# VectorE takes all element-wise work of a two-block network kernel from GpSimd; rotary tables and feed-forward operands are made at other places

## The chip, the cores and the metric

The kernel runs on one core of one Trainium2 chip: TensorE (PE, matrix products into PSUM), VectorE (DVE), ScalarE (ACT), GpSimd (POOL), and SyncE (SP), which issues most DMAs. The metric is the device time of one execution in microseconds, the median of several.

## The reference

Everything is fp32, with 512 tokens of width 1024. Cut to what matters (`first_block` is two layers, then `second_block` once):

```python
for l in range(2):
    x = x + 0.5 * swiglu(rmsnorm(x, g_ffn1[l]), wg1[l], wu1[l], wd1[l])      # d_ff = 2816
    u = rmsnorm(x, g_mix[l]); p = u @ w_in[l]
    y_a, y_b, y_c = fourier(p), dilated_attention(p), diff_attention(p)
    x = x + (gates(u) * (y_a, y_b, y_c)).sum() @ w_out[l]
    x = x + 0.5 * swiglu(rmsnorm(x, g_ffn2[l]), wg2[l], wu2[l], wd2[l])
x = rmsnorm(x, g_final)
# second block
proj = rms_norm(x, g_mix_pre) @ w_in_2
attn = window_attention(rope(aq), rope(ak), av)          # 8 heads, 2 kv heads
q, k, v = silu(conv5(dqkv)); q, k = l2norm(q), l2norm(k)  # 4 heads of 128
dn = gated_delta(q, k, v, g, beta) + flip(gated_delta(flip(q, k, v, g, beta)))
x = x + rms_norm([attn, gated(dn)] @ w_out_2, g_mix_post)
x = x + rms_norm(cross_attention(rms_norm(x), rms_norm(mem)), g_cross_post)
x = x + rms_norm(swiglu2(rms_norm(x, g_ffn_pre)), g_ffn_post)
```

## The kernel before, in words

The activations lie transposed: `self.x[c]`, c = 0 to 7, holds 128 channels x 512 tokens. Each fp32 product is made of three matmuls: every operand is split into a rounded part `hi` and a rest `lo` (`split`: ScalarE copies `hi`, VectorE subtracts to get `lo`), and hi·hi, hi·lo and lo·hi are summed in PSUM. Weights come as slabs of 512 KB (`raw`), are split in the same way into `whi` and `wlo`, and TensorE takes them in order.

The kernel is written as tasks (Python generators). `drive` picks the next task by priority and due time; `note` keeps an estimated clock for each engine (per instruction 0.065 + 0.00105 n us on VectorE, 0.17 + 0.00075 n on ScalarE, 0.1 + 0.0027 n on GpSimd, n the elements of a partition) and `when` gives the estimated time at which a tile is done. So the order of each engine's instructions comes from these estimates, and an instruction that is given to another engine moves others too. Each engine then works through its own list in order. One helper records every operation, so that all rows of the profile have one line, L119; the names tell them apart: `g` is any general tile of 128x512, `sm` a small one, `ps` a PSUM bank.

Places that the change touches:

- `split_w` (line 310) splits weight slabs. While `pool_w` is on (second mixer and cross attention), every second `lo` is subtracted on GpSimd.
- `sq_pool` (464) sums squares for a norm: at each new chunk of x a square (ScalarE) and an addition (GpSimd).
- `ffn_task` (821): hidden tiles 0 to 5 are made the plain way, tiles 6 to 21 by a fast scheme that makes a 2x2 block product from seven smaller ones. Its x operands 1 to 7 come from `fast_ops` (722): eight subtractions `g<-b` or `g<-b,g`, each split, in one go between the hidden tiles 4 and 5.
- `setup_second` (1389) makes the rotary tables `sin` and `cos` from the positions after the fourth feed-forward's fast part (`rooms == 4`), beside the chunks of the norm after it (`pre_chunk` with `G_FINAL`).
- `final_norm` (1440): finishes that norm, then multiplies the 8 chunks of x by 1/rms on GpSimd and stores them.
- In `mixer2_task` (1646), `conv`: for q and v heads two of five taps go over ScalarE and GpSimd. `gs` is the decay strength of the gated delta rule, which TensorE needs for cumulative sums (`strengths`); `l2_heads` normalises the K heads (`g<-ps,sm`).
- `delta_k`, `delta` and `rope` have multiplications on GpSimd; so have `post_task`, `post_halves` (norms after the mixer and the cross attention) and `finish`.
- `memory_proj` (2312) loads the normed memory from `mem_d` over GpSimd's DMA queue and starts its product 5 us (planner's time) later.

Of the kernel before, what the change touches and what calls it, by code (L numbers as in the profile page):

```python
# [135 lines left out]
class Net:  # L136
    def __init__(self, ctx, tc, ins, dump=None):
# [21 lines left out]
        self.pool_w = self.turn = False  # L159
# [161 lines left out]
    def slab(self, src, kc, c, whole=False):  # L321
# [142 lines left out]
    def sq_pool(self, k, x):  # L464
# [7 lines left out]
        if k == len(self.acc):  # L472
            self.acc.append(q)
        else:
            nc.gpsimd.tensor_tensor(self.acc[k], self.acc[k], q, ALU.add)

    def wide(self, srcs, us, first=4):
# [4 lines left out]
        for k in range(KC):  # L482
            if k % 4 == 0:
                self.lock, self.ahead = self.cur, True
                n = first if k == 0 else 4
                for j, src in enumerate(srcs):
# [235 lines left out]
    def fast_ops(self, xn, xr):  # L722
# [3 lines left out]
        ops = [None] * 8  # L726
        for i, r, sl in ((1, 0, one), (2, 1, one), (3, 1, two)):
            ops[i] = [(xr[2 * k + r][0][:, sl], xr[2 * k + r][1][:, sl]) for k in range(KC // 2)]
        for i in (4, 5, 6, 7):
            ops[i] = []  # L730
        for q in range(2):
            b11, b12, b21, b22 = (xn[r][q][:, :, sl] for r in range(2) for sl in (one, two))
            t = []
            for i, a, b in ((5, b12, b11), (6, b22, None), (7, b22, b12), (4, b21, None)):
                b = t[(i == 4)] if b is None else b
                t.append(self.g(shape=[P, 2, 256]))
                sub(a, b)
                hi, lo = self.split(t[-1], self.g(F32R, [P, 2, 256]), self.g(F32R, [P, 2, 256]))
                ops[i] += [(hi[:, k], lo[:, k]) for k in range(2)]
        return ops  # L740
# [80 lines left out]
    def ffn_task(self, wg, wu, wd, pre, row, after):  # L821
# [31 lines left out]
        xs = self.fast_ops(xn, xr)  # L853
# [32 lines left out]
        down(0, 6, (0,))  # L886
        load(0)
# [501 lines left out]
    def setup_second(self):  # L1389
# [27 lines left out]
        k = self.g()
        big = 12582912.0
        nc.vector.tensor_scalar(k, ang, 1.0 / (2.0 * math.pi), big, ALU.mult, ALU.add)
        nc.vector.tensor_scalar_add(k, k, -big)  # L1420
        c1 = 6.28125
        c2 = math.floor((2.0 * math.pi - c1) * 2.0 ** 20) / 2.0 ** 20
        c3 = 2.0 * math.pi - c1 - c2
        for c in (c1, c2, c3):
            nc.vector.scalar_tensor_tensor(ang, k, -c, ang, ALU.mult, ALU.add)
        nc.vector.tensor_scalar(k, ang, 1.0 / (2.0 * math.pi), big, ALU.mult, ALU.add)
        nc.vector.tensor_scalar_add(k, k, -big)
        for c in (c1, c2 + c3):
            nc.vector.scalar_tensor_tensor(ang, k, -c, ang, ALU.mult, ALU.add)
        lim = 3.1415925  # L1430
        nc.vector.tensor_scalar(ang, ang, -lim, lim, ALU.max, ALU.min)
        self.sin = self.pcst([P, S], "sin")
        nc.scalar.activation(self.sin, ang, AF.Sin)
        nc.vector.tensor_scalar_mul(self.sin, self.sin, self.m_sgn)
        nc.scalar.activation(ang, ang, AF.Abs)
        nc.vector.tensor_scalar(ang, ang, -1.0, 0.5 * math.pi, ALU.mult, ALU.add)
        self.cos = self.pcst([P, S], "cos")
        nc.scalar.activation(self.cos, ang, AF.Sin)

    def final_norm(self, a1, a2):  # L1440
# [19 lines left out]
        for c in range(KC):  # L1460
            nc.gpsimd.tensor_tensor(self.x[c], self.x[c], r1b, ALU.mult)
# [5 lines left out]
    def post_task(self, row, res, nxt, done):  # L1467
# [13 lines left out]
        for c in range(1, KC, 2):  # L1481
            nc.gpsimd.tensor_tensor(ms[c], ms[c], rb, ALU.mult)
# [55 lines left out]
    def post_halves(self, row, res, nxt, half, done):  # L1538
# [22 lines left out]
        def chunks(n, cs, p=None):  # L1561
            sl = slice(256 * n, 256 * n + 256)
            for c in cs:
                if c % 2:
                    nc.gpsimd.tensor_tensor(ms[c][:, sl], ms[c][:, sl], rbs[n], ALU.mult)
            for c in cs:
# [32 lines left out]
    def wide_halves(self, srcs):  # L1599
# [5 lines left out]
        for k in range(0, KC, 4):  # L1605
            w.append([])
            for j, src in enumerate(srcs):
# [3 lines left out]
                for c in range(2):  # L1611
# [5 lines left out]
                    w[-1].append(self.split_w(raw[:, :, c * P:(c + 1) * P], hi, lo))  # L1617
# [28 lines left out]
    def mixer2_task(self, after):  # L1646
# [6 lines left out]
        self.pool_w = True  # L1653
# [15 lines left out]
        def conv(p, x, h):  # L1669
# [997 lines left out]
```

## Time and profile before

| | us |
|---|---|
| median of 3 runs | 3449.83 (3449.82 to 3457.95) |
| profiled execution | 3453.07 |
| its span | 3451.3 |
| TensorE busy | 3320.4 (96%), x19063 |
| VectorE busy | 2297.5 (67%), x4180 |
| ScalarE busy | 1572.5 (46%), x3064 |
| GpSimd busy | 360.2 (10%), x372, 241 of them two-operand arithmetic |

TensorE's matmuls are 83% of the chain that ended last. The stretches that the text speaks of: the first feed-forward up to 172 us; mixers and feed-forwards to 2408; the last down product of the fourth feed-forward, the norm after it and the first product of the second mixer to 2494; the second mixer to 2924; its norm and the cross attention to 3096; the last feed-forward to the end. In a timeline the arrow names what ended an engine's wait; "x4" at a row means four like instructions in a row, and the time is that of all four.

### The profile page before, as it was taken

To read this page: it belongs to the slowest core of one execution; us is meant where nothing else is said; L and a number is where in the kernel's file an instruction comes from. 1 tells how busy PE (TensorE), PEld (TensorE's weight loads), DVE (VectorE), ACT (ScalarE), POOL (GpSimd) and SP (SyncE) were. 2 spreads that over 40 slices of the span, in tenths; PEclk is the share of its full clock that TensorE was granted. 3 is DMA by queue.
4 is the path that set the end of the run, shared out by engine and by line. 5 is a ranking of instruction groups with operands and counts; after the bars stand their busy time and mean duration, and the time that the engine had idled before them with its cause. 6 is when DMAs were issued, how large, how long until landed. Compare 5 with 4: busy or idle time off the path is not lost.

```text
span 3451.3 us, 50657 instructions
## 1 busy us (share of the span) xinstructions
PE 3320.4 (96%) x19063; PEld 2910.4 (84%) x19063; DVE 2297.5 (67%) x4180; ACT 1572.5 (46%) x3064; POOL 360.2 (10%) x372
## 2 busy tenths in 40 slices
PE   8899999999999999999999999999879888999998
PEld 6799888898899988998888988999667877888887
DVE  5677677656577777776775566777778674754344
ACT  4354545443444554544454434445454254443232
POOL 2000100000100010001000000000454412220001
PEclk9999999999999999999999999999989999999999
DMA  4443332435333333333333357333255623223332
GB/s 131 129 128 92 117 96 92 133 106 181 95 104 108 110 113 107 111 92 117 94 97 119 115 182 141 116 97 97 73 185 171 204 62 104 68 74 99 96 98 73
DMA packets 370949, 391.03 MB, mean 113 GB/s; under 512 B 30801, under 2 KB 325309, under 8 KB 370704
## 3 DMA queue, kind: packets, MB, share of 16 engines
q1 hardware_dynamic: 329248, 332.45, 32.1%
q10 hardware_dynamic: 38464, 47.68, 4.9%
q0 software_dynamic: 2992, 7.67, 0.7%
q8 instruction: 149, 2.44, 0.3%
q14 instruction: 96, 0.79, 0.1%
HBM read 343.56 MB, written 39.98 MB: 111 GB/s over the span
## 4 chain that ended last, share of the span: by engine, by line
PE 83%; DVE 7%; issue 2%; DMA 2%; ACT 1%; POOL 1%; SPq 0%; ACTq 0%; DVEq 0%; POOLq 0%
PE ps L119 83%; DVE g L119 5%; ACT g L119 1%; DVE wlo L119 1%; DVE sm L119 1%; DMA g<-cs_d 0%; POOL g L119 0%; DMA g<-g 0%; DMA g<-xinv_d 0%; SPq L119 0%; DVE tmp L119 0%; DMA b<-in_w_ffn_up 0%; ACT whi L119 0%; DMA g<-mem_d 0%; DMA g<-bias_d 0%
## 5 line engine op out<-in xcount | busy, mean ns | idle before, releaser
L119 PE MATMUL ps<-g,whi 128*128 128x512 f32 (+1 forms) x9312 | 2418.1, 350 | 36.3 <-ACT g L119 20.4
L119 PEld LDWEIGHTS ps<-g,whi 128*128 128x128 f32 x9312 | 1626.7, 191 | 259.8 <-ACT g L119 26.5
L119 PE MATMUL ps<-g,wlo 128*128 128x512 f32 (+1 forms) x4656 | 1619.4, 348 | 14.3 <-DVE wlo L119 14.1
L119 ACT ACTIVATE whi<-raw 128x512 fp32r<-128x512 f32 (+1 forms) x1084 | 669.7, 622 | 881.0 <-PE ps L119 786.5
L119 PEld LDWEIGHTS ps<-g,wlo 128*128 128x128 f32 x4656 | 888.7, 191 | 126.8 <-DVE wlo L119 16.5
L119 DVE TENSOR_TENSOR wlo<-raw,whi 128x512 fp32r<-128x512 f32 (+1 forms) x1022 | 704.0, 696 | 391.9 <-ACT whi L119 376.2
L119 ACT ACTIVATE g<-g 128x256 fp32r<-128x256 f32 (+4 forms) x561 | 311.5, 571 | 217.2 <-DVE g L119 182.1
L119 DVE TENSOR_TENSOR g<-g,g 128x512 f32<-128x512 f32 (+4 forms) x550 | 349.3, 655 | 88.7 <-ACT g L119 78.2
L119 POOL TENSOR_TENSOR g<-g,g 128x512 f32<-128x512 f32 (+3 forms) x142 | 179.6, 1273 | 1571.0 <-ACT g L119 1467.2
L119 DVE TENSOR_TENSOR g<-ps,g 128x512 f32<-128x512 f32 (+3 forms) x350 | 204.3, 598 | 197.0 <-PE ps L119 99.6
L119 PE MATMUL ps<-g,g 128*128 128x128 f32 (+5 forms) x1638 | 268.2, 312 | 23.7 <-DVE g L119 11.4
L119 PEld LDWEIGHTS ps<-g,g 128*128 128x128 f32 (+3 forms) x1638 | 226.5, 195 | 46.1 <-DVE g L119 11.5
L119 PE MATMUL ps<-whi,g 128*128 128x256 f32 (+1 forms) x1184 | 256.9, 310 | 0.1
L119 ACT ACTIVATE whi<-b 128x512 fp32r<-128x512 f32 x192 | 121.2, 632 | 223.6 <-PE ps L119 212.5
L119 DVE SCALAR_TENSOR_TENSOR g<-ps,g 128x512 f32<-128x512 f32 x210 | 149.1, 711 | 105.5 <-PE ps L119 103.4
L119 PEld LDWEIGHTS ps<-whi,g 128*128 128x128 f32 x1184 | 196.8, 192 | 11.8 <-ACT whi L119 0.4
L119 PE MATMUL ps<-wlo,g 128*128 128x256 f32 (+1 forms) x592 | 183.8, 311 | 5.8 <-DVE wlo L119 4.8
L119 DVE TENSOR_TENSOR wlo<-b,whi 128x512 fp32r<-128x512 f32 x192 | 131.8, 688 | 55.1 <-ACT whi L119 54.5
L119 ACT COPY g<-ps 128x512 f32<-128x512 f32 (+5 forms) x250 | 114.0, 476 | 118.2 <-PE ps L119 105.8
L119 ACT ACTIVATE g<-ps 128x256 fp32r<-128x256 f32 (+6 forms) x239 | 100.5, 430 | 144.3 <-PE ps L119 126.2
L119 DVE TENSOR_TENSOR g<-g,ps 128x512 f32<-128x512 f32 (+1 forms) x171 | 111.4, 656 | 40.7 <-PE ps L119 34.8
L119 PEld LDWEIGHTS ps<-wlo,g 128*128 128x128 f32 x592 | 113.6, 192 | 12.5 <-DVE wlo L119 5.6
(201 smaller groups left out, 1849.7 us busy)
## 6 DMA issues: line engine op xcount, KB each, us to landing
raw<-in_w_ffn_down SPq DMA_DIRECT2D x80, 512.0 KB, 3.5
raw<-in_w_in SPq DMA_DIRECT2D x80, 512.0 KB, 3.9
raw<-in_w_ffn_gate SPq DMA_DIRECT2D x55, 512.0 KB, 3.9
raw<-in_w_ffn_up SPq DMA_DIRECT2D x55, 512.0 KB, 4.4
raw<-in_w_gate SPq DMA_DIRECT2D x48, 512.0 KB, 3.7
raw<-in_w_gate_up SPq DMA_DIRECT2D x44, 512.0 KB, 3.6
b<-in_w_ffn_gate SPq DMA_DIRECT2D x32, 512.0 KB, 3.8
b<-in_w_ffn_up SPq DMA_DIRECT2D x32, 512.0 KB, 3.9
```

What stands on the lines that cost most here:

```text
L119: r = f(*a, **k)
```

## The change

All element-wise work of GpSimd goes to VectorE: `split_w` is replaced by `split`, and the additions and multiplications of the functions above are written for `nc.vector`. GpSimd keeps memsets and DMA issues. The convolutions of q and v heads do all five taps as K heads did (one ScalarE scaling, four VectorE multiply-adds). `fast_ops` makes its operands in two calls, the first at the old place, the second as an item of the list of the fast scheme, behind the first down slab. The rotary tables are made during the fourth feed-forward, in the tiles `sin` and `cos` themselves, a few instructions every 8 us of the planner's time. `memory_proj` waits 20 us instead of 5 between its loads and its product. The core of the diff:

```diff
-    def split_w(self, src, hi, lo):
-        self.nc.scalar.activation(hi, src, AF.Copy)
-        self.turn = self.pool_w and not self.turn
-        (self.nc.gpsimd if self.turn else self.nc.vector).tensor_tensor(lo, src, hi.bitcast(F32), ALU.subtract)
-        return hi, lo
...
-            self.split_w(q[4], hi, lo)
+            self.split(q[4], hi, lo)
...
-            nc.gpsimd.tensor_tensor(self.acc[k], self.acc[k], q, ALU.add)
+            nc.vector.tensor_tensor(self.acc[k], self.acc[k], q, ALU.add)
...
-        xs = self.fast_ops(xn, xr)
+        xs = [[] for _ in range(8)]
+        self.fast_ops(xn, xr, xs, 0)
         evac(5, self.proj_t(sg, P, xr), self.proj_t(su, P, xr), False)
...
         down(0, 6, (0,))
+        items.append((lambda: self.fast_ops(xn, xr, xs, 1), None))
         load(0)
...
-        yield lambda: self.rooms == 4
-        pi = self.g(I32)
-        nc.gpsimd.dma_start(pi, i["positions_2"][0].partition_broadcast(P))
-        yield 16.0
+        ang, k = self.pcst([P, S], "sin"), self.pcst([P, S], "cos")
+        nc.gpsimd.dma_start(k.bitcast(I32), i["positions_2"][0].partition_broadcast(P))
+        yield 40.0
...
+            yield 8.0
+            nc.vector.tensor_scalar(k, ang, 1.0 / (2.0 * pi), big, ALU.mult, ALU.add)
...
         for c in range(KC):
-            nc.gpsimd.tensor_tensor(self.x[c], self.x[c], r1b, ALU.mult)
+            nc.vector.tensor_tensor(self.x[c], self.x[c], r1b, ALU.mult)
...
-            for j in (1, 3) if pool else (0, 1, 3, 4):
+            for j in (0, 1, 3, 4):
...
-        nc.gpsimd.tensor_tensor(v3(rv), v3(rv), be3, ALU.mult)
-        nc.gpsimd.tensor_tensor(v3(kg), v3(kg), self.b3(self.kgs[c]), ALU.mult)
+        nc.vector.tensor_tensor(v3(rv), v3(rv), be3, ALU.mult)
+        nc.vector.tensor_tensor(v3(kg), v3(kg), self.b3(self.kgs[c]), ALU.mult)
...
-        yield 5.0
+        yield 20.0
         w = i["w_ckv_2"][0]
```

VectorE's list in the first feed-forward, before: `g_845<-ps_820,g_845` is the product of the hidden tile f = 5, `b_490` and `b_492` are normed x, the `g<-b` rows with the rows `g<-g,g` after them are the subtractions and splits of `fast_ops`.

```order
L119 TENSOR_TENSOR g_780<-g_777,g_779 128x512
L119 TENSOR_TENSOR g_783<-b_492,b_490 128x512
L119 TENSOR_SCALAR bgh<-par 128x48
L119 TENSOR_SCALAR slg<-par 128x1 x2
L119 TENSOR_TENSOR g_786<-g_783,g_785 128x512
L119 TENSOR_TENSOR g_789<-b_492,g_777 128x512
L119 TENSOR_TENSOR wlo_911<-raw_900,whi_910 128x512
L119 TENSOR_TENSOR g_792<-g_789,g_791 128x512
L119 TENSOR_TENSOR wlo_915<-raw_890,whi_914 128x512
L119 TENSOR_TENSOR g_845<-ps_820,g_845 128x512
L119 TENSOR_TENSOR g_850<-g_845,g_849 128x512
```

The same place after; `g_821<-ps_796,g_821` is the product of f = 5 here, and `g_866<-b_490` the first row of the second step.

```order
L119 TENSOR_TENSOR g_768<-g_765,g_767 128x512
L119 TENSOR_TENSOR wlo_903<-raw_898,whi_902 128x512
L119 TENSOR_TENSOR raw_894<-raw_894,b_896 128x1024
L119 TENSOR_TENSOR g_821<-ps_796,g_821 128x512
L119 COPY par<-ps_829 128x128
L119 TENSOR_TENSOR wlo_907<-raw_898,whi_906 128x512
L119 TENSOR_TENSOR g_826<-g_821,g_825 128x512
L119 TENSOR_SCALAR bgh<-par 128x48
L119 TENSOR_TENSOR g_835<-g_740 128x256
L119 TENSOR_SCALAR slg<-par 128x1 x2
L119 TENSOR_REDUCE sm_837<-g_835 128x4
L119 TENSOR_TENSOR g_866<-b_490 128x512
```

The product was behind all subtractions; it now stands behind the first four and ahead of the second four.

VectorE's list beside the fourth feed-forward's last chunks, before (`g_20842` and its neighbours are chunks of x, `g_24766` and `g_24769` the rotary angles, `gain` the norm's weight):

```order
L119 SCALAR_TENSOR_TENSOR g_20844<-ps_24812,g_20844 128x512
L119 TENSOR_SCALAR g_24769<-g_24769 128x512
L119 TENSOR_SCALAR g_20842<-g_20842,gain 128x512
L119 SCALAR_TENSOR_TENSOR g_24766<-g_24769,g_24766 128x512 x2
L119 SCALAR_TENSOR_TENSOR g_24806<-g_20842,gain,g_24805 128x512
L119 SCALAR_TENSOR_TENSOR g_24766<-g_24769,g_24766 128x512
L119 TENSOR_SCALAR g_20844<-g_20844,gain 128x512
L119 TENSOR_SCALAR g_24769<-g_24766 128x512
L119 SCALAR_TENSOR_TENSOR g_20846<-ps_24837,g_20846 128x512
L119 TENSOR_SCALAR g_24769<-g_24769 128x512
L119 SCALAR_TENSOR_TENSOR g_24831<-g_20844,gain,g_24830 128x512
```

After, for the same chunks; `g_24707` and `g_24700` are the two sums of squares, which GpSimd held before:

```order
L119 SCALAR_TENSOR_TENSOR g_20846<-ps_24834,g_20846 128x512
L119 TENSOR_TENSOR wlo_24912<-raw_24905,whi_24911 128x512
L119 SCALAR_TENSOR_TENSOR g_24803<-g_20842,gain,g_24802 128x512
L119 TENSOR_TENSOR g_24707<-g_24707,g_24806 128x512
L119 TENSOR_TENSOR g_24700<-g_24700,g_24823 128x512
L119 TENSOR_SCALAR g_20844<-g_20844,gain 128x512
L119 SCALAR_TENSOR_TENSOR g_20848<-ps_24859,g_20848 128x512
L119 TENSOR_TENSOR wlo_24918<-raw_24915,whi_24917 128x512
L119 SCALAR_TENSOR_TENSOR g_24828<-g_20844,gain,g_24827 128x512
```

The rotary rows are gone from this place (they stand among rows of the fourth feed-forward), and two sums of squares a chunk have come.

VectorE's list at `gs`, before:

```order
L119 TENSOR_TENSOR z<-z,nea 128x32
L119 SCALAR_TENSOR_TENSOR g_25208<-g_25152,par,g_25208 128x510
L119 COPY gs<-z 128x32
L119 SCALAR_TENSOR_TENSOR g_25196<-g_25150,par,g_25196 128x511
L119 SCALAR_TENSOR_TENSOR g_25208<-g_25152,par,g_25208 128x511
L119 TENSOR_SCALAR gn<-ps_25256 128x32
L119 SCALAR_TENSOR_TENSOR g_25196<-g_25150,par,g_25196 128x511
```

After, where `g_20834` to `g_20848` are the eight chunks of x that `final_norm` multiplies; GpSimd had these rows:

```order
L119 TENSOR_TENSOR z<-z,nea 128x32
L119 SCALAR_TENSOR_TENSOR g_25169<-g_25143,par,g_25169 128x510
L119 COPY gs<-z 128x32
L119 SCALAR_TENSOR_TENSOR g_25193<-g_25147,par,g_25193 128x510
L119 TENSOR_TENSOR g_20834<-g_20834,g_25227 128x512
...
L119 TENSOR_TENSOR g_20848<-g_20848,g_25227 128x512
L119 TENSOR_SCALAR gn<-ps_25253 128x32
L119 SCALAR_TENSOR_TENSOR g_25163<-g_25141,g_25163 128x512
L119 TENSOR_TENSOR beg<-beg,beta 128x32
```

The eight multiplications stand between `gs` and `gn`.

## Rows read from the trace of the kernel before

**Rows 1.** windows; per engine busy us (x instructions), then TensorE's clock
```profile
core 0: us, PE busy (x) PEld busy (x) DVE busy (x) ACT busy (x) POOL busy (x), PEclk, DMA share, GB/s
86.00:172.00 86.00, 75.46 (x422) 63.41 (x421) 59.70 (x96) 33.62 (x57) 3.52 (x8) 0.92 0.44 129
172.00:2408.00 2236.00, 2229.75 (x13324) 1984.29 (x13324) 1557.13 (x2747) 1081.80 (x2033) 70.94 (x102) 1.00 0.39 114
2408.00:2494.00 86.00, 74.51 (x348) 59.22 (x347) 61.84 (x97) 36.74 (x66) 30.44 (x21) 0.94 0.23 68
2494.00:2666.00 172.00, 142.19 (x785) 122.62 (x784) 144.04 (x271) 87.27 (x222) 92.28 (x90) 0.90 0.56 168
2666.00:2924.00 258.00, 222.92 (x1457) 198.03 (x1455) 149.90 (x399) 98.13 (x244) 77.41 (x63) 0.93 0.43 133
2924.00:3096.00 172.00, 157.20 (x861) 136.96 (x862) 116.22 (x214) 83.27 (x187) 51.02 (x42) 0.92 0.21 67
```

**Rows 2.** lines by form, VectorE: 1292:1548 (first row), 2424:2666; count, busy us, mean ns
```profile
L119 DVE TENSOR_TENSOR wlo<-raw,whi 128x512 fp32r<-128x512 f32 x98 | 67.0, 689 | 32.2 <-ACT whi L119 31.2
...
L119 DVE TENSOR_TENSOR wlo<-raw,whi 128x512 fp32r<-128x512 f32 x36 | 35.7, 993 | 14.9 <-ACT whi L119 14.6
L119 DVE TENSOR_TENSOR g<-ps,g 128x512 f32<-128x512 f32 x26 | 17.2, 683 | 2.8 <-ACT g L119 2.8
```

**Rows 3.** timeline of VectorE around POOL's run; start, duration, row, idle before and releaser
```profile
2497.17 0.17 DVE L119 TENSOR_SCALAR ez<-ez 128x32 f32<-128x32 f32 x1
...
2504.09 1.79 DVE L119 SCALAR_TENSOR_TENSOR g<-g,par,g 128x510 f32<-128x510 f32 x1
...
2508.69 1.24 DVE L119 COPY gs<-z 128x32 f32<-128x32 f32 x1
...
2545.64 0.69 DVE L119 TENSOR_TENSOR g<-ps,sm 128x512 f32<-128x512 f32 x1
```

**Rows 4.** timeline of TensorE, first feed-forward
```profile
108.27 1.22 PE L119 MATMUL ps<-g,whi 128*128 128x512 f32 x2 [9.20 <-ACT g L119]
```

**Rows 5.** timeline of VectorE, first feed-forward
```profile
98.37 1.23 DVE L119 TENSOR_TENSOR raw<-raw,b 128x1024 f32<-128x1024 f32 x1 [1.13 <-DMA b<-in_w_ffn_up]
...
106.87 0.68 DVE L119 TENSOR_TENSOR g<-ps,g 128x512 f32<-128x512 f32 x1
```

**Rows 6.** a window of TensorE after that wait; busy us, clock
```profile
112.00:116.00 4.00, 4.00 (x9) 0.50 0.08 15
```

**Rows 7.** timeline of TensorE, first product of the second mixer
```profile
2448.37 2.08 PE L119 MATMUL ps<-g,whi 128*128 128x512 f32 x4 [2.78 <-ACT whi L119]
...
2461.51 0.80 PE L119 MATMUL ps<-g,wlo 128*128 128x512 f32 x1 [7.75 <-DVE wlo L119]
```

**Rows 8.** timeline of VectorE in the same stretch
```profile
2439.69 1.52 DVE L119 CAST g<-g 128x512 f32<-128x512 int32 x1
...
2459.70 1.75 DVE L119 TENSOR_TENSOR wlo<-raw,whi 128x512 fp32r<-128x512 f32 x1
```

**Rows 9.** timeline of TensorE after that product
```profile
2509.99 0.64 PE L119 MATMUL ps<-gs,ones 128*128 128x32 f32 x2 [9.69 <-DVE gs L119]
...
2534.44 1.21 PE L119 MATMUL ps<-g,whi 128*128 128x256 f32 x2 [6.65 <-DMA g<-mem_d]
```

**Rows 10.** timeline of POOL
```profile
2497.80 12.09 POOL L119 TENSOR_TENSOR g<-g,g 128x512 f32<-128x512 f32 x8 [1.76 <-ACT g L119]
...
2531.39 4.30 POOL L119 DMA_DIRECT2D g<-mem_d  x8
```

**Rows 11.** timeline of TensorE, delta rule
```profile
2810.30 2.07 PE L119 MATMUL ps<-g,g 128*128 128x128 f32 x8 [6.76 <-DVE g L119]
```

**Rows 12.** timeline of VectorE after the mixer
```profile
2920.70 6.77 DVE L119 TENSOR_TENSOR g<-g,g 128x512 f32<-128x512 f32 x4 [0.67 <-POOL g L119]
```

**Rows 13.** timeline of TensorE after the mixer
```profile
2924.92 2.08 PE L119 MATMUL ps<-g,whi 128*128 128x512 f32 x4 [4.80 <-ACT g L119]
2929.20 0.80 PE L119 MATMUL ps<-g,whi 128*128 128x512 f32 x1 [2.21 <-DVE g L119]
```

More of the change, by code (lines that the diff above doesn't have):

```diff
@@ L495, in wide @@
                         for k0 in range(0, 4, n):
-                            self.split_w(raw[:, k0:k0 + n, c * P:(c + 1) * P], hi[:, k0:k0 + n], lo[:, k0:k0 + n])
+                            self.split(raw[:, k0:k0 + n, c * P:(c + 1) * P], hi[:, k0:k0 + n], lo[:, k0:k0 + n])
                         w[2 * j + c] = hi, lo
@@ L720, in fast_x, with fast_ops @@
         return xn, xr
-    def fast_ops(self, xn, xr):
+    def fast_ops(self, xn, xr, ops, q):
         sub = lambda a, b: self.nc.vector.tensor_tensor(t[-1], a, b, ALU.subtract)
         one, two = slice(0, 256), slice(256, S)
-        ops = [None] * 8
         for i, r, sl in ((1, 0, one), (2, 1, one), (3, 1, two)):
[L728 to L740, printed above, removed]
+            ops[i] += [(xr[2 * k + r][0][:, sl], xr[2 * k + r][1][:, sl]) for k in (2 * q, 2 * q + 1)]
+        b11, b12, b21, b22 = (xn[r][q][:, :, sl] for r in range(2) for sl in (one, two))
+        t = []
+        for i, a, b in ((5, b12, b11), (6, b22, None), (7, b22, b12), (4, b21, None)):
+            b = t[(i == 4)] if b is None else b
+            t.append(self.g(shape=[P, 2, 256]))
+            sub(a, b)
+            hi, lo = self.split(t[-1], self.g(F32R, [P, 2, 256]), self.g(F32R, [P, 2, 256]))
+            ops[i] += [(hi[:, k], lo[:, k]) for k in range(2)]
     def fast_load(self, wg, wu, f):
@@ L1416, in setup_second @@
+        nc.vector.tensor_copy(ang, k.bitcast(I32))
         nc.vector.tensor_scalar_mul(ang, ang, self.m_freq)
[L1417 to L1420, printed above, removed]
         c1 = 6.28125
[L1422 to L1429, printed above, removed]
+        c2 = math.floor((2.0 * pi - c1) * 2.0 ** 20) / 2.0 ** 20
+        c3 = 2.0 * pi - c1 - c2
+        for cs in ((c1, c2, c3), (c1, c2 + c3)):
+            yield 8.0
+            nc.vector.tensor_scalar(k, ang, 1.0 / (2.0 * pi), big, ALU.mult, ALU.add)
+            nc.vector.tensor_scalar_add(k, k, -big)
+            for c in cs:
+                yield 8.0
+                nc.vector.scalar_tensor_tensor(ang, k, -c, ang, ALU.mult, ALU.add)
@@ L1440, in final_norm @@
+        nc.scalar.activation(ang, ang, AF.Sin)
+        yield 8.0
+        nc.vector.tensor_scalar_mul(ang, ang, self.m_sgn)
+        nc.vector.tensor_scalar(k, k, -1.0, 0.5 * pi, ALU.mult, ALU.add)
+        nc.scalar.activation(k, k, AF.Sin)
+        self.sin, self.cos = ang, k
     def final_norm(self, a1, a2):
@@ L1583, in chunks @@
                     nc.scalar.activation(q, x, AF.Square)
-                    eng = nc.vector if c % 2 and n else nc.gpsimd
-                    eng.tensor_tensor(self.acc[0][:, sl], self.acc[0][:, sl], q, ALU.add)
+                    nc.vector.tensor_tensor(self.acc[0][:, sl], self.acc[0][:, sl], q, ALU.add)
         p = yield from norm(0)
@@ L1616, in wide_halves @@
                         lo = self.wlo.tile([P, 4, P], F32R, tag="wlo", name=self.nm("wlo"))
-                    w[-1].append(self.split_w(raw[:, :, c * P:(c + 1) * P], hi, lo))
+                    w[-1].append(self.split(raw[:, :, c * P:(c + 1) * P], hi, lo))
         self.ahead = False
@@ L1753, in mixer2_task @@
             self.spawn(self.solve_task(half, st), 1)
-        self.pool_w = True
         for x in (0, 2):
@@ L1915, in delta_k @@
             self.kgs[c] = self.pcst([P, NT], f"kgs{c}")
-            nc.gpsimd.tensor_copy(self.kgs[c], v3(dt)[:, :, last])
+            nc.vector.tensor_copy(self.kgs[c], v3(dt)[:, :, last])
             self.dt[c] = dt
             lt = self.g()
-            (nc.vector if d else nc.gpsimd).tensor_tensor(lt, dt, kkm, ALU.mult)
+            nc.vector.tensor_tensor(lt, dt, kkm, ALU.mult)
             yield self.when(lt)
```

44 lines of the change are left out of this document (12 added, 32 removed).

## The prediction

> **What bounds the kernel now.** I read the page first: TensorE is busy 96% of a span of 3451.3 us and its matmuls are 83% of the chain of waits, so only time in which TensorE stands still, or runs at its lower clock, can be won. Cut into stretches [rows 1], that time is not spread out. From 172 to 2408 TensorE is busy 2229.75 of 2236 us at clock 1.00: three feed-forwards and two mixers there offer at most 6.3 us. The other stretches have 10.5 us (86:172), 11.5 (2408:2494), 29.8 (2494:2666), 35.1 (2666:2924) and 14.8 (2924:3096), and a clock of 0.90 to 0.94. Then I read the timeline of TensorE for the idle times in these stretches, and of VectorE and GpSimd (POOL) beside them for what was late.
>
> What makes VectorE late shows in a comparison of one instruction [rows 2]: the low half of a weight split, `wlo<-raw,whi`, takes 689 ns in a stretch where POOL does nothing, and 993 ns on average in 2424:2666 where POOL computes. Beside it `g<-ps,g`, of which one operand is in PSUM, stays at 683. Single rows of the two-operand kind take 1.75 to 1.79 us [rows 3], about what one of them and one of POOL's 1.4 us rows take in a row. So an instruction given to POOL costs VectorE up to 1.1 us each time the two meet, against 0.69 us (0.61 from start to start of neighbours) for doing it itself. The Trainium skill, "SBUF — State Buffer", section "Who interferes with whom", says that VectorE and GpSimd hold a shared port pair as an exclusive lock for a whole instruction, that a VectorE instruction with two SBUF inputs contends with a GpSimd one that reads SBUF, and that one with at most one SBUF input does not. The 993 beside the 683 agree. By the rule every such wait goes; the fourth rival below says what that gives.
>
> **First feed-forward: the operands in two steps.** TensorE waits 9.20 us before 108.27 for the hidden tile f = 5 [rows 4]. Its product `g<-ps,g` runs on VectorE only at 106.87 [rows 5], behind all eight subtractions and splits. In the new order it stands ahead of the second four, directly behind `raw<-raw,b`, which waits for a DMA and ends at 98.37 + 1.23 = 99.6 [rows 5]. TensorE followed 1.40 us after the product's start (108.27 - 106.87), so it would go on at about 101.0 to 101.5 and wait some 2.3 us instead of 9.2: 7 us. After the wait TensorE ran at a granted clock of 0.50, the 1.2 GHz level, to 116 at least [rows 6], nearly 8 us of which half are lost; with a shorter wait I expect half of these 4 us back: 2. Term: **-9** (ends -11 and -5). The second step's work is as much as before and stands beside two down slabs. The three later feed-forwards have no such wait (the 6.3 us above), and I cost them at nothing.
>
> **Rotary tables and the start of the second mixer, 2408 to 2494.** The 11.5 us are three waits, 0.95, 2.78 and 7.75 us, the last two in [rows 7], for a `whi` and for the `wlo` of 2459.70. VectorE is not idle then: between two chunks' evacuations it does the rotary angles (14 rows, of which CAST with 1.52 us is the first [rows 8]; about 13 us with their waits for POOL) and its own rows are stretched (`wlo` 1.75 [rows 8], against 0.69). The change takes those 13 us out. It adds 13 squares' sums and 4 `wlo` that POOL had, 17 x 0.61 = 10.4, and gives back about 10 rows x 1 us of waits for POOL. VectorE reaches the last `wlo` some 13 us earlier. The waits and what the lower clock cost (0.06 of 86 us is 5; some 3 of it, I estimate, while matmuls ran) are 14.5 together. Term: **-12.5** (ends -14.5 and -4). The rotary rows now lie in the fourth feed-forward, in a stretch whose VectorE is busy 1557 of 2236 us [rows 1], which hides them; were that cover gone, some 8 us unblocked. ScalarE's three table functions go with them.
>
> **From there to the K heads.** TensorE waits 9.69 us for `gs` [rows 9]. POOL does eight multiplications in one run of 12.09 us from 2497.80 [rows 10]; beside it five wide rows of VectorE take 1.75 to 1.79 and three tiny ones 1.25 (`gs<-z`: 1.24; `ez`, as small, is 0.17 just before POOL's run [rows 3]). That is 5 x 1.05 + 3 x 1.08 = 8.5 us that go. The eight multiplications then stand on VectorE right behind `gs` and ahead of `gn`, 8 x 0.61 = 4.9 us, so 2 to 3 us of wait stay. Behind them VectorE has more to do: up to the fourth K head's `g<-ps,sm` 50 wide rows and 41 small ones follow `gs` (27 and 41 before), at 0.64 and 0.19 us that is 40 us without a pause, where it took 2545.64 - 2508.69 = 37.0 before [rows 3]: 3.5 us more, and TensorE waits for these heads. The 6.65 us for `mem_d` [rows 9] go out of the chain, since the eight DMAs that stood behind POOL's rows until 2531.39 [rows 10] are issued early; but TensorE would otherwise wait for VectorE there. Term: -8.5 + 3.5 = **-5**, ends -16 (the 6.65 and the clock too) and +8.5 (the 23 moved rows are paid in full at 0.64, and 6 us come back elsewhere).
>
> **Delta rule, window attention, 2580 to 2924.** POOL's 63 instructions of 2666:2924 [rows 1] come to VectorE: 63 x 0.69 = 43 us on 149.9 busy of 258, of which it idles 108. Its rows here are blocked less (6.76 us before 2810.30 [rows 11] is one place where TensorE waits for such a chain), so I give back 8 to 10. Products `beta`, `kgs` stood beside VectorE's own and now stand in its queue. The page shows no such queue before; bounds are -10 (all the blocked time was on the path) and +34 (every moved row is). By the average 70% load I take the nearer one: **+4**. The convolutions lose two ScalarE scalings and gain two VectorE rows a head; those are in the 50 above.
>
> A rule of the Trainium skill speaks against all this: "Perfetto Trace Analysis", section "Optimizing Scalar/DVE Operations", says that when VectorE is saturated, giving work to GpSimd may make sense, though it adds that the two share a port and it might not help. VectorE's 144.04 us of 172 in 2494:2666 look saturated; the rows that take 1.75 for 0.69 say that part of it is waiting. By the rule the sum would come out as in the second rival.
>
> **Between mixer, cross attention and the last feed-forward.** VectorE's four multiplications from 2920.70 take 6.77 us while POOL does its four [rows 12], and TensorE waits 4.80 and 2.21 us [rows 13]. Eight rows alone are 8 x 0.61 = 4.9 before the first gain row instead of 6.8, and the later rows of 1.75 become 0.75: of 9.8 us of waits up to 2946 I take half. Term **-5** (ends -9.8 and 0). The halves of the cross attention wait 2 to 2.5 us three times; **-2**. The last feed-forward's few rows count nothing.
>
> **Sum.** -9 - 12.5 - 5 + 4 - 5 - 2 = -29.5 on the profiled execution's 3453.07: 3423.6. That execution is 3.2 above the median of the runs, so the forecast is **3420**.
>
> **Rivals.** (1) Given back later: the K heads and the delta rule are a chain through VectorE, and being 21 us early (12.5 + 8.5) only lets it meet its queue earlier. For: VectorE is 84% busy in 2494:2666, and 23 more wide rows before the fourth K head. Against: a good part of that 84% is waiting. Left are -9 - 5 - 2: 3437, as a median 3434; with the first term at -5, 3440. (2) Slower: VectorE's in-order queue becomes the bound from `gs` to 2924. Price: 23 rows x 0.64 = 14.7 in place of 3.5 (nothing blocked comes back), and +34 for the delta rule; 48.7 less 9 + 12.5 + 8.5 + 5 + 2 = 37 gives +12: 3465. It decides once VectorE has no idle time between K heads and the state updates; the 108 us idle of 258 speak against it. (3) POOL is not what stretches VectorE's rows: then nothing is given back, each stretch gets its moved rows on top, and the time is well over 3470; rows 2 speak against it. (4) More: all waits for POOL were on the path. Then -9, -12.5, -16 up to the K heads, -10 in the delta rule, -9.8 and -2: -59, 3391 as a median. The rule of the Trainium skill on SBUF, named above, would give this if each wait that it explains counts. For it: TensorE idles 91 us in 2408:3096; against: most of the 35 in 2666:2924 lie in chains that alternate between engines.
>
> **How the numbers follow.** Forecast 0.50 (its own range 3408 to 3432), rival 1 0.23, rival 2 0.06, rival 3 0.02, rival 4 0.19. The range 3398 to 3446 holds the forecast, nearly all of rival 1, and half of rival 4. What a measurement of this kernel tells from no change is 0.3%, 10.35 us: faster is below 3439.5, slower above 3460.2. Faster: the forecast, rival 4 and two thirds of rival 1: 0.83. Same: a third of rival 1 and the edge of rival 2: 0.10. Slower: 0.07.
>
> **What would show it.** In the profile after: the wait before the sixth hidden tile of the first feed-forward 2 to 3 us; none over 2 us in the second mixer's first product; POOL with no computing rows but memsets; `wlo` at 0.69 everywhere; the wait at `gs` 2 to 3 us; TensorE's idle time in the delta rule about as before; VectorE's busy sum (2297.5 before) higher by less than the 241 x 0.69 = 166 us that come, by what the stretched rows give back. I am wrong if `wlo` still has long rows, or if new waits for `g<-ps,sm` at the K heads sum to more than 15 us.

## The result and the profile after

The changed kernel takes 3402.46 us (median of 4 runs, 3396.84 to 3412.0) against 3449.82 before: ratio 0.986, 95% interval 0.9833 to 0.9887. That is 47 us less, where 29.5 were forecast; the time lies in the stated range of 3398 to 3446, but 5.5 us below the forecast's own of 3408 to 3432. The profiled execution took 3396.84 us, the shortest of the four.

The page and five windows of the changed kernel (columns as in [rows 1]; the stretches are shifted to hold about the same work):

```profile
PE 3295.8 (97%) x19063; PEld 2895.3 (85%) x19063; DVE 2325.5 (68%) x4423; ACT 1562.3 (46%) x3049; POOL 45.2 (1%) x121
```

```profile
86.00:163.00 77.00, 71.82 (x410) 61.05 (x409) 56.56 (x92) 32.99 (x54) 3.00 (x7) 0.96 0.49 143
...
2404.00:2474.00 70.00, 69.70 (x325) 55.19 (x323) 50.44 (x106) 36.89 (x64) 4.70 (x8) 1.00 0.33 106
2474.00:2630.00 156.00, 133.17 (x782) 117.81 (x783) 135.64 (x330) 70.71 (x196) 3.68 (x8) 0.91 0.64 194
2630.00:2884.00 254.00, 218.23 (x1429) 192.71 (x1427) 172.78 (x460) 99.81 (x246) 0.00 (x0) 0.95 0.39 119
2884.00:3040.00 156.00, 149.47 (x870) 131.89 (x871) 109.31 (x253) 83.57 (x188) 0.00 (x0) 0.98 0.24 78
```

TensorE no longer waits in the second mixer's first product (0.3 us of 70, clock 1.00). VectorE got 243 instructions more, yet its busy sum rose by 28 us only, not by the 166 that 241 x 0.69 come to. The line by form that answers to [rows 2], VectorE in 2412:2640 of the changed kernel:

```profile
L119 DVE TENSOR_TENSOR wlo<-raw,whi 128x512 fp32r<-128x512 f32 x71 | 47.5, 686 | 11.6 <-ACT whi L119 11.5
```

It is 686 ns here; in a stretch without GpSimd it was 689 before. At `gs`, VectorE, then TensorE of the changed kernel (answering to [rows 3, 9]):

```profile
2472.83 0.18 DVE L119 TENSOR_TENSOR z<-z,nea 128x32 f32<-128x32 f32 x1
...
2473.59 0.18 DVE L119 COPY gs<-z 128x32 f32<-128x32 f32 x1
...
2474.54 4.90 DVE L119 TENSOR_TENSOR g<-g,g 128x512 f32<-128x512 f32 x8
...
2512.34 0.69 DVE L119 TENSOR_TENSOR g<-ps,sm 128x512 f32<-128x512 f32 x1
```

```profile
2473.82 0.41 PE L119 MATMUL ps<-gs,ones 128*128 128x32 f32 x2 [0.30 <-DVE gs L119]
...
2479.60 0.39 PE L119 MATMUL ps<-ident,gn 128*32 128x128 f32 x1 [3.81 <-DVE gn L119]
...
2498.76 0.66 PE L119 MATMUL ps<-ident,g 128*128 128x128 f32 x4 [3.56 <-DVE g L119]
2506.84 2.08 PE L119 MATMUL ps<-g 128*128 128x128 f32 x8 [7.42 <-ACT g L119]
...
2512.43 1.16 PE L119 MATMUL ps<-g 128*128 128x128 f32 x8 [2.66 <-ACT g L119]
```

The tiny rows are 0.18 instead of 1.24, and TensorE waits 0.30 us for `gs` where it waited 9.69. New waits follow: 3.81 us at `gn`, behind the eight multiplications, and 13.6 us at the K heads (3.56 + 7.42 + 2.66). From `gs` to the fourth K head VectorE took 2512.34 - 2473.59 = 38.8 us; the forecast had 40.

To see where the time went I matched the two traces by the start of the same matmul (the n-th one with a `whi` or `wlo` operand, the first being number 0; `gs` by its own row). e9 is a run of the next section.

| point | before, us | after, difference | e9, difference |
|---|---|---|---|
| first matmul with a weight | 17.58 | -0.9 | +0.1 |
| 300th, just before the wait for f = 5 | 94.83 | -3.2 | -2.2 |
| 360th, after it | 123.03 | -8.1 | -2.1 |
| 12600th, shortly before the second mixer | 2414.92 | -11.2 | -1.4 |
| `gs` | 2509.99 | -36.2 | -26.2 |
| 13760th, end of the second mixer | 2917.16 | -39.6 | -40.6 |
| 14390th, cross attention done | 3110.24 | -56.6 | -56.7 |
| last | 3420.25 | -57.1 | -56.7 |

Of the profile's 57 us some 3 lie in the first 95 us, which differ by up to 4 between executions of like code; the medians' 47 hold less of that. Each column is one execution. Up to the end of the second mixer e11 (of the next section) has the changed kernel's instructions in the same order, yet it took 409.9 us from `gs` to that end, at a clock of 0.91 in the delta rule, where the changed kernel took 403.8 at 0.95. So a difference of less than some 6 us in this stretch between two traces says nothing.

### The profile page after: what moved, and what is told of

It is laid out like the page before. It is cut to its first block, busy times and chain, and to the rows that moved or that the text cites. A ratio compares the mean times of both kernels' runs of the same rounds, so it can differ in the third digit from the quotient of the medians.

```text
span 3395.1 us, 50388 instructions
## 1 busy us (share of the span) xinstructions
PE 3295.8 (97%) x19063; PEld 2895.3 (85%) x19063; DVE 2325.5 (68%) x4423; ACT 1562.3 (46%) x3049; POOL 45.2 (1%) x121
## 4 chain that ended last, share of the span: by engine, by line
PE 89%; DVE 7%; DMA 2%; ACT 1%; issue 1%; SPq 0%; ACTq 0%; DVEq 0%; POOL 0%; POOLq 0%
PE ps L119 89%; DVE g L119 5%; ACT g L119 1%; DVE wlo L119 1%; DMA b<-in_w_ffn_up 0%; DVE sm L119 0%; DMA g<-xinv_d 0%; DMA g<-in_x 0%; DVE b L119 0%; DMA g<-cs_d 0%; ACT whi L119 0%; DVE tmp L119 0%; DMA g<-in_g_ffn 0%; DVE xs L119 0%; SPq L119 0%
## 5 line engine op out<-in xcount | busy, mean ns | idle before, releaser
L119 DVE TENSOR_TENSOR wlo<-raw,whi 128x512 fp32r<-128x512 f32 (+1 forms) x1084 | 726.6, 678 | 392.7 <-ACT whi L119 377.7
L119 DVE TENSOR_TENSOR g<-g,g 128x512 f32<-128x512 f32 (+4 forms) x668 | 401.7, 622 | 74.6 <-ACT g L119 64.8
L119 ACT ACTIVATE g<-g,sm 128x512 f32<-128x512 f32 (+3 forms) x160 | 89.3, 579 | 37.0 <-DVE sm L119 36.0
```

Source lines behind the costliest of these rows:

```text
L119: r = f(*a, **k)
```

## The experiments

Ratios are to the kernel before on the same chip, in five rounds each. e1 to e3 take the change apart.

**e1**, the kernel before with the operands in two steps alone:

```diff
-        xs = self.fast_ops(xn, xr)
+        xs = [[] for _ in range(8)]
+        self.fast_ops(xn, xr, xs, 0)
...
+        items.append((lambda: self.fast_ops(xn, xr, xs, 1), None))
```

> The kernel before with one part of the change alone: the feed-forward operands in two steps. My account: the wait of 9.20 us before the sixth hidden tile falls to 2 to 5 us, the later parts of the kernel stay as they are, so 5 to 9 us less than before, about 3442. Rival (the second step stands in the way later, or the wait has another cause): the time of before within 3 us.

3445.51 us, ratio 0.9978 (0.9968 to 0.9987): 4.5 to 11 us less. My account holds. In its trace, the wait fell from 9.20 to 5.06 us:

```profile
97.55 1.53 PE L119 MATMUL ps<-g,whi 128*128 128x512 f32 x2 [5.06 <-ACT g L119]
```

**e2**, the kernel before with the rotary tables alone moved:

```diff
-        yield lambda: self.rooms == 4
-        pi = self.g(I32)
...
+        ang, k = self.pcst([P, S], "sin"), self.pcst([P, S], "cos")
+        yield 40.0
```

> The kernel before with the rotary tables alone moved into the fourth feed-forward; GpSimd keeps all its work. My account: VectorE loses 14 rows and some 13 us between the last chunks, so the waits of 11.5 us in the second mixer's first product shrink to 0 to 4 us and the time falls by 8 to 12 us, to about 3440. Rival (the waits come from GpSimd's blocking, not from the rotary rows): 0 to 4 us less. Rival (given back at the wait for gs, which GpSimd's run of 12 us sets): the waits go, the one for gs grows by as much, and the time is that of before.

3457.11 us, 1.0013 (1.0004 to 1.0021): slower by 1 to 7 us. TensorE of e2:

```profile
2449.63 1.22 PE L119 MATMUL ps<-g,whi 128*128 128x512 f32 x2 [3.76 <-ACT whi L119]
2452.08 0.80 PE L119 MATMUL ps<-g,wlo 128*128 128x512 f32 x1 [1.22 <-DVE wlo L119]
...
2504.40 0.64 PE L119 MATMUL ps<-gs,ones 128*128 128x32 f32 x2 [10.22 <-DVE gs L119]
```

The waits of the first product shrank from 11.5 to 5 us as I expected, and the one for `gs` stayed at 10. So `gs` came 5.6 us earlier, but the mixer ended 6.9 us later: with the planner's new order, TensorE waits five times for 3 to 6 us between 2808 and 2868, by its rows for the window heads (`ps<-ident,g` behind ScalarE). The third guess (given back) is right in the sum, though not at the wait for `gs`.

**e3**, the change without these two parts:

```diff
-        self.fast_ops(xn, xr, xs, 0)
+        xs = self.fast_ops(xn, xr)
...
+        yield lambda: self.rooms == 4
+        pi = self.g(I32)
```

> The changed kernel with the other two parts undone: operands in one go, rotary tables at the old place; GpSimd does no element-wise work and the memory product starts 20 instead of 5 planned us after its loads. My account: what is left of the gain of 47 us without the two parts is 26 to 34, about 3419. Rival (the gain comes from the two moves, GpSimd's work costs VectorE as much as it spares it): 0 to 10 less than before.

3418.04 us, 0.9899 (0.9884 to 0.9914): 35 us less. Most of the gain is GpSimd's part. In its trace TensorE is busy without a break from 2404 to `gs`, which comes 32.1 us earlier than before; half of that is lost by the mixer's end (16.8 us earlier), with waits like those of e2 (5.79, 5.68, 3.00 and 5.02 us by `ps<-ident,g`).

e4 to e6 put useless rows on GpSimd; PE, VectorE and ScalarE keep the changed kernel's instructions and order.

**e4**, 62 reading rows:

```diff
+        if self.turn:
+            self.nc.gpsimd.tensor_copy(self.dz[:, 0:1], hi[:, 0, 0:1].bitcast(F32))
+            self.nc.gpsimd.tensor_tensor(self.dz[:, 1:S], self.dz[:, 1:S], self.dz[:, 1:S], ALU.mult)
```

> The changed kernel with 62 extra rows on GpSimd, one at every second weight split of the second mixer and the cross attention, each a two-operand product on a private tile of zeros (128x511) that nobody uses, behind a copy of one column of whi that times it. PE, VectorE and ScalarE have the same instructions in the same order as in the changed kernel. My account (a GpSimd row that reads SBUF blocks VectorE's two-operand rows for its duration): VectorE's rows there get to 0.85 to 1.0 us on average, and the time rises by 8 to 25 us over the changed kernel. Rival (VectorE's long rows had another cause than GpSimd): VectorE's rows stay at 0.69 and the time is that of the changed kernel within 5 us.

3436.69 us, 0.9955 (0.9942 to 0.9968). The products did not wait for the copies, which write another column: they ran in one stretch beside the fourth feed-forward. POOL's timeline, then VectorE's lines by form in 1970:2060, TensorE's timeline and the window:

```profile
1960.70 80.59 POOL L119 TENSOR_TENSOR dz<-dz 128x511 f32<-128x511 f32 x61
```

```profile
L119 DVE TENSOR_TENSOR g<-g,g 128x512 fp32r<-128x512 f32 x17 | 20.8, 1238 | 1.9 <-ACT g L119 1.8
...
L119 DVE TENSOR_TENSOR wlo<-raw,whi 128x512 fp32r<-128x512 f32 x15 | 15.0, 1019 | 0.0
...
L119 DVE SCALAR_TENSOR_TENSOR g<-g,ps 128x512 f32<-128x512 f32 x21 | 13.8, 676 | 0.0
...
L119 DVE TENSOR_SCALAR cos<-cos 128x512 f32<-128x512 f32 x3 | 2.8, 941 | 0.0
```

```profile
2029.22 0.79 PE L119 MATMUL ps<-g,wlo 128*128 128x512 f32 x1 [8.22 <-DVE wlo L119]
```

```profile
1970.00:2060.00 90.00, 69.68 (x261) 53.63 (x259) 87.28 (x97) 25.26 (x49) 67.14 (x54) 0.87 0.42 135
```

A stretch in which TensorE hardly waits otherwise lost some 31 us (the same matmuls, before and behind it). VectorE is busy 87 of 90 us, its two-operand rows take 1.0 to 1.24 us, and the row with a PSUM operand stays at 0.68. What makes this place so dear shows in the windows of the same 158 matmuls and 67 VectorE rows, in the changed kernel and in e4:

```profile
1965.40:2000.70 35.30, 35.30 (x158) 29.22 (x157) 34.78 (x67) 15.03 (x32) 0.00 (x0) 1.00 0.71 230
```

```profile
1970.00:2036.70 66.70, 46.38 (x158) 34.34 (x157) 66.63 (x67) 14.87 (x33) 62.78 (x51) 0.82 0.37 120
```

VectorE was already busy 34.8 of 35.3 us there, so all that its rows grew (31.8 us) came out as time. The rival (another cause) falls; the place was not the one meant.

**e5**, the same rows tied to their places:

```diff
-            self.nc.gpsimd.tensor_tensor(self.dz[:, 1:S], self.dz[:, 1:S], self.dz[:, 1:S], ALU.mult)
+            self.nc.gpsimd.tensor_tensor(self.dz, self.dz, self.dz, ALU.mult)
```

> As the run with 62 useless reading rows on GpSimd, but each product now also takes the column that the copy before it has written, so that it can't run ahead of its weight split: the 62 rows (copy of one column of whi, then dz = dz * dz, 128x512) stand beside the second mixer and the cross attention. PE, VectorE and ScalarE keep the changed kernel's order. In the run before this one the same 62 rows ran in one stretch of 80 us beside the fourth feed-forward, VectorE's rows there took 1.0 to 1.24 us instead of 0.69, and 34 us were lost. My account (reading rows block VectorE's two-operand rows): wlo goes from 0.69 to 0.85 to 1.0 us, and the time is 10 to 30 us over the changed kernel, 3412 to 3432. Rival (only a long stretch without a pause hurts): within 4 us of the changed kernel.

**e6**, memsets instead:

```diff
-            self.nc.gpsimd.tensor_tensor(self.dz, self.dz, self.dz, ALU.mult)
+            for _ in range(2):
+                self.nc.gpsimd.memset(self.dz, 0.0)
```

> As the kernel with 62 useless products in place, with two memsets of the same private tile (128x512, about 0.5 us each) in place of each product; the copies of one column stay. GpSimd is busy at the same places for about as long, but its long rows read nothing. My account (what blocks is the reading, not that GpSimd is busy): VectorE's wlo stays at 0.69 to 0.72 and the time is within 4 us of the changed kernel. Rival (any GpSimd row blocks): wlo at 0.85 to 1.0 and 8 to 25 us more, as with the products.

e5 took 3415.22 us, 0.9887 (0.987 to 0.9903), e6 3403.75, 0.9854 (0.9838 to 0.987): 11 us apart, and e6 is the changed kernel within its interval. Lines by form in 2400:3100, VectorE and POOL of e5, then of e6:

```profile
L119 DVE TENSOR_TENSOR wlo<-raw,whi 128x512 fp32r<-128x512 f32 x155 | 112.4, 735 | 67.2 <-ACT whi L119 66.7
```

```profile
L119 POOL TENSOR_TENSOR dz<-dz 128x512 f32<-128x512 f32 x62 | 78.9, 1273 | 5.0
```

```profile
L119 DVE TENSOR_TENSOR wlo<-raw,whi 128x512 fp32r<-128x512 f32 x159 | 107.9, 687 | 72.5 <-ACT whi L119 72.1
```

```profile
L119 POOL MEMSET dz<- 128x512 f32 x124 | 65.9, 531 | 7.1
```

GpSimd's memsets, which only write, leave VectorE at 687 (so do the copies of one column beside them, which e5 has too); its products, which read 512 columns, do not. The mean of 735 is below the 850 that I expected, since not every split meets a product, and still 11 us are lost.

**e7**, the 62 rows of the delta rule and the rotation back on GpSimd, planned as such:

```diff
-        nc.vector.tensor_tensor(v3(rv), v3(rv), be3, ALU.mult)
-        nc.vector.tensor_tensor(v3(kg), v3(kg), self.b3(self.kgs[c]), ALU.mult)
+        nc.gpsimd.tensor_tensor(v3(rv), v3(rv), be3, ALU.mult)
+        nc.gpsimd.tensor_tensor(v3(kg), v3(kg), self.b3(self.kgs[c]), ALU.mult)
...
```

> The changed kernel with the delta rule's and the rotation's products back on GpSimd (62 rows: the masks by beta, rv by beta, kg by kgs, the query decay, four lt, kgs, and rotation's two), all other work on VectorE. The prediction's account (on VectorE these rows cost 4 us net): 0 to 8 us less than the changed kernel. The rival that the result speaks for (in the stretch 2580 to 2924 the kernel gained about 13 us where +4 was forecast, so these rows blocked more than they spared): 5 to 15 us more than the changed kernel.

3416.03 us, 0.9891 (0.9871 to 0.991), some 11 us over the changed kernel. That looked like the rival, but the planner had made another order too; **e10** keeps the changed kernel's plan and only issues the rows to GpSimd (the order stays nearly the same: 155 matmuls of TensorE stand at other places, against 1348 in e7):

```diff
+        self.other = Engine(net, nc.gpsimd, "vector")
...
-        nc.vector.tensor_tensor(v3(rv), v3(rv), be3, ALU.mult)
+        nc.other.tensor_tensor(v3(rv), v3(rv), be3, ALU.mult)
...
```

> The changed kernel and its plan (VectorE's clock and costs), with the 62 rows of the delta rule and the rotation issued to GpSimd. With the planner's own view of GpSimd the same rows cost some 11 to 14 us over the changed kernel. Account A (blocking and GpSimd's longer rows in the chains cost it): 8 to 16 us over the changed kernel here too. Rival B (the other order cost it): within 4 us of the changed kernel.

3403.87 us, 0.9856 (0.984 to 0.9871): the changed kernel, within the interval. VectorE of e10, lines by form in 2640:2890:

```profile
L119 DVE TENSOR_TENSOR g<-g,g 64x512 fp32r<-64x512 f32 x10 | 9.8, 982 | 0.4
...
L119 DVE TENSOR_TENSOR g<-g,beg 128x512 f32<-128x512 f32 x8 | 7.7, 958 | 0.0
```

Its rows are stretched (the 64x512 ones take 686 in the changed kernel), but the end does not move. So these rows' engine is worth too little to be told from nothing, and e7's loss is mostly its order.

**e8**, the eight multiplications later:

```diff
-        yield 6.0
+        yield 30.0
         r1b = self.rowsb(r1)
```

> The changed kernel with the eight multiplications of the final norm 30 instead of 6 planned us after their scale, so that they no longer stand on VectorE between gs and gn and ahead of the K heads. My account (VectorE's list is the bound from gs to the K heads, where TensorE now waits 3.81 us at gn and some 14 us at the K heads): 4 to 8 us less than the changed kernel, 3395 to 3398. Rival (the rows come due later in the same queue, or the eight tiles held longer delay others): within 3 us of the changed kernel, or more.

3401.3 us, 0.9845 (0.9828 to 0.9862): not told apart from the changed kernel, so the 4 to 8 us that I expected are not there. The wait at `gn` is gone from its trace (0.36 us), three later waits stay (4.58 + 4.72 + 3.29 = 12.6 us), and the mixer ends no earlier after its `gs`: 405.2 us (2478.84 to 2884.08) for the changed kernel's 403.8 (2473.82 to 2877.58).

**e9**, the kernel before with its own plan, VectorE executing GpSimd's rows; operands and rotary tables untouched:

```diff
+        self.other = Engine(net, nc.vector, "gpsimd")
...
-            nc.gpsimd.tensor_tensor(self.acc[k], self.acc[k], q, ALU.add)
+            nc.other.tensor_tensor(self.acc[k], self.acc[k], q, ALU.add)
...
```

> The kernel before, its planner left as it was (it still takes GpSimd's clock and costs for these rows), but every element-wise row that it plans for GpSimd is issued to VectorE; operands in one go and rotary tables at the old place. So the order is nearly that of before and only the engine that computes differs. Account A (the gain is the chip's: no blocking, and shorter rows than GpSimd's in the chains): 25 to 40 us less than before, 3410 to 3425, most of it behind 2408. Rival B (a good part of the gain comes from the new order that the planner makes when it no longer has GpSimd): 0 to 15 us less than before.

3398.16 us, 0.9846 (0.9832 to 0.9859): 53 us less than before, more than account A had and as fast as the full change. The order is nearly that of before (314 of 19063 matmuls stand elsewhere). VectorE at the place of [rows 8], and the window there:

```profile
2437.90 0.42 DVE L119 CAST g<-g 128x512 f32<-128x512 int32 x1
2438.24 0.68 DVE L119 TENSOR_TENSOR wlo<-raw,whi 128x512 fp32r<-128x512 f32 x1
2438.84 0.48 DVE L119 TENSOR_SCALAR g<-g,m_freq 128x512 f32<-128x512 f32 x1
```

```profile
2408.00:2482.00 74.00, 74.00 (x366) 59.63 (x365) 61.24 (x126) 40.41 (x72) 4.33 (x8) 1.00 0.35 107
```

The rotary rows stand where they stood and TensorE does not wait at all. In the first feed-forward its wait is as before, 8.82 us. e3 leaves the same two parts undone and has GpSimd as silent, yet it lies 18 us above e9 (0.9899 against 0.9846). The two differ in the planner's order, the convolutions' taps and the start of the memory product, and which of these it is was not run apart. With its two moves on top of e3 the full change comes back to e9's time, not below it.

**e11**, post_task and post_halves back on GpSimd:

```diff
         for c in range(1, KC, 2):
-            nc.vector.tensor_tensor(ms[c], ms[c], rb, ALU.mult)
+            nc.gpsimd.tensor_tensor(ms[c], ms[c], rb, ALU.mult)
...
```

> The changed kernel with the rows of post_task and post_halves back on GpSimd (four multiplications of the norm after the mixer, and the halves' multiplications and sums of squares after the cross attention), weight splits and all else on VectorE. The prediction's account gave these places 7 us together; the profile after shows 17 us gained from 2917 of before on. If these rows are the cause: 8 to 17 us over the changed kernel. Rival (the 17 us come from the weight splits of the cross attention, which stay on VectorE here): 0 to 5 us over it.

3411.78 us, 0.9885 (0.9871 to 0.9899), 9 us over the changed kernel by the medians, 7.6 of them in the traces between the mixer's end and the end of the cross attention. VectorE after the mixer, in the changed kernel and in e11 (the row of [rows 12]):

```profile
2879.77 2.50 DVE L119 TENSOR_TENSOR g<-g,g 128x512 f32<-128x512 f32 x4 [0.27 <-ACT g L119]
```

```profile
2889.22 5.68 DVE L119 TENSOR_TENSOR g<-g,g 128x512 f32<-128x512 f32 x4 [0.68 <-POOL g L119]
```

About half of the 17.5 us of these stages comes from these rows.

**e12**, two further moves (that of e8 and this one):

```diff
-        self.fast_ops(xn, xr, xs, 0)
         evac(5, self.proj_t(sg, P, xr), self.proj_t(su, P, xr), False)
         yield 0
+        self.fast_ops(xn, xr, xs, 0)
```

> The changed kernel with two further moves: the final norm's eight multiplications 30 instead of 6 planned us after their scale (alone that was -3 to 0 us), and the first half of the feed-forward operands behind the hidden tile f = 5 instead of ahead of it, so that the product of tile 5 no longer waits for any of them. My account: the wait of 5.02 us before 97.5 in the first feed-forward falls under 2 us and 3 to 6 us go, 3394 to 3399. Rival (the operands then come late for the first of the seven products, or the wait is one for weights): within 3 us of the changed kernel, or slower.

3399.86 us, 0.9847 (0.9833 to 0.9861): not told apart from the changed kernel. The wait for tile 5 is gone; TensorE waits at the first of the seven products instead:

```profile
113.38 0.50 PE L119 MATMUL ps<-g,whi 128*128 128x256 f32 x2 [1.65 <-ACT g L119]
...
115.86 0.58 PE L119 MATMUL ps<-g,wlo 128*128 128x256 f32 x1 [1.98 <-DVE wlo L119]
```

The fastest kernels are thus the changed one, e8, e9 and e12, not told apart. e9 with the two steps of e1 would be their sum, about 3390 us (3398.2 - 7.6), as an estimate; it was not run.

## Why the prediction was right, and where its sizes were off

**Mechanism.** Right, and shown: GpSimd's reading rows stretch VectorE's two-operand rows (e4, e5, with e6 as the control), and with them gone the kernel is faster even under the old plan (e9). The third rival falls with that. The Trainium skill, "SBUF — State Buffer", section "Who interferes with whom", says the same of the shared port pair, that only a GpSimd instruction which reads SBUF meets a two-input VectorE one; e6's 687 against e5's 735 agree. For rows with one SBUF input that section of the Trainium skill is narrower than the prediction's sentence on it: it says that they don't contend outside the 2-port performance modes, a condition that the prediction left out; the CAST with 1.52 us beside GpSimd [rows 8] and 0.42 in e9 is a row with one SBUF input that was stretched. The Trainium skill's hint on a saturated VectorE ("Perfetto Trace Analysis", section "Optimizing Scalar/DVE Operations") does not carry here: VectorE's 144 of 172 us were waiting in good part, and taking GpSimd's help away won time.

**First feed-forward, -9.** 5 us between the 300th and the 360th matmul, 7.6 in e1's ratio. The wait is 5.02 us, not 2.3: I took TensorE's last work before the wait to end at the old place. In the new order the wait comes 15 weight matmuls, 3.4 us, earlier in TensorE's list (number 303 instead of 318), while the row in front of the product, which waits for a DMA, comes only 0.2 us earlier, counted from the 300th matmul (94.98 - 91.66 against 98.37 - 94.83). The changed kernel's TensorE, then its VectorE:

```profile
97.52 1.53 PE L119 MATMUL ps<-g,whi 128*128 128x512 f32 x2 [5.02 <-ACT g L119]
```

```profile
94.98 1.23 DVE L119 TENSOR_TENSOR raw<-raw,b 128x1024 f32<-128x1024 f32 x1 [1.70 <-DMA b<-in_w_ffn_up]
96.12 0.68 DVE L119 TENSOR_TENSOR g<-ps,g 128x512 f32<-128x512 f32 x1
```

The 2 us for the clock did not come either: after the shorter wait it was 0.50 too, from 97.5 to 104 (6.5 us, where it had been some 8), which gives back under 1 us. So 4.2 + 0.8 = 5.0 stand for 7 + 2.

**Rotary tables, -12.5, and `gs`, -8.5.** The sum is met (21 forecast, 25 measured from the 12600th matmul to `gs`), the reason of the first is wrong. The waits were those of rotary rows that GpSimd stretched, and silencing GpSimd is enough: with the rows left in place and GpSimd silent they are gone (e9, e3), and with the rows moved and GpSimd at work 5 of 11.5 us stay and nothing is won in the end (e2). VectorE had room for 14 rows of 0.4 to 0.7 us; it had none for rows of 1.5 to 1.75. I had counted 13 us for the rows "with their waits for POOL" and so booked GpSimd's share under the move.

**K heads, +3.5, and delta rule, +4.** From `gs` to the end of the mixer 7.5 us were to be lost. The changed kernel won 3.4 (39.6 - 36.2); the same instructions in e11 lost 2.7, so 5 to 11 us of the forecast's loss did not come; e9 won 14.4. VectorE's list up to the fourth K head was well sized (38.8 us for 40, 1.8 more than before), and TensorE's new waits there, 13.6 us, stay under the 15 that I had named. What failed is the delta rule's term, the step "63 x 0.69 = 43 us on 149.9 busy" with 8 to 10 given back: VectorE's busy time there rose by 22.9 us only, from 149.90 [rows 1] to 172.78, so 20 came back from its other rows, and TensorE idles 35.8 us where it idled 35.1. I charged these rows to VectorE's queue, but VectorE still idles a third of this stretch, and e10 shows no loss or gain from who executes them (1.4 us by the medians; 4.8 from `gs` to the end of the mixer in the traces, less than the 6 between two executions of like instructions). The order alone moved the end by some 12 us (e7 against e10). How the rest of the 17.5 us between forecast and measurement divides is open. The second rival, whose price was built on the same charge, falls, and so does the first: of the 25 us nothing was given back, or the 2.7 of e11.

**Norms and cross attention, -5 and -2.** 17.5 measured. e11 gives some 9 of them to the rows that I had counted. The rest I had left out: it is consistent with the weight splits of the cross attention, which GpSimd had stretched too (the kernel before, VectorE's lines by form in 2924:3096). That was not run by itself; the useless reads of e5 beside these splits cost 3.5 us from the mixer's end to the end of the cross attention (e5 won 13.6 us there on the kernel before, e6 17.1). Some 5 us stay open.

```profile
L119 DVE TENSOR_TENSOR wlo<-raw,whi 128x512 fp32r<-128x512 f32 x24 | 20.7, 865 | 18.7 <-ACT whi L119 18.7
```

**Sum.** Forecast and measured, on the profile: up to the second mixer -9 and -11.2, to `gs` -21 and -25.0, to the mixer's end +7.5 and -3.4, behind it -7 and -17.5; together -29.5 and -57.1, the medians' -47. The fourth rival (3391) was nearer to the median than the forecast (3420). Yet not every wait for GpSimd had been on the path: VectorE's rows got shorter by some 138 us in all (166 - 28, as an estimate), of which 47 reached the end.

Two numbers of the prediction don't come out, without touching the forecast: a row of 0.69 and one of 1.4 us in a row make 2.1, not 1.75 to 1.79, and rival 1 with the first term at -5 is 3441 on the profile and 3438 as a median, not 3440.

## What to carry to other kernels

Before pricing work that moves off GpSimd, compare one VectorE instruction's duration with GpSimd silent and at work: the stretched rows are the price, and they show as VectorE's load, not as waiting. They cost most where VectorE has no idle time left, whatever its average over the kernel. Where several causes meet in one wait, test each alone; the one that looks busiest (here the rotary rows) may be free. Where a planner orders the work, keep its plan and change only the executing engine before crediting an edit: here the order alone moved as much as many edits.

## What the runs showed of the hardware that was not expected

The same 62 reading GpSimd rows cost 31 us in one place (e4) and 11 spread over others (e5). In the first, TensorE had no idle time and VectorE was busy 34.8 of 35.3 us, though over 172 to 2408 it is busy 70% [rows 1]; its rows there grew by 31.8 us. Rows with one SBUF operand are stretched too: CAST took 1.52 us beside GpSimd and 0.42 without, `cos<-cos` 0.94 in e4 and 0.42 in the changed kernel. GpSimd's copy of a single column took 0.56 us on average in e6.
